# Which engine clears, rotates and sums, and when weights are split at the seams of a two-block network

## The chip, the core and the metric

The kernel runs on one core of one Trainium2 chip. Four engines compute: TensorE (PE, matmuls), VectorE (DVE), ScalarE (ACT) and GpSimd (POOL); SyncE (SP) issues most of the DMAs that bring the weights. The metric is the device time of one execution in microseconds (us). Three runs of the kernel before took 1218.33, 1220.27 and 1220.82 us.

## The reference, cut to what matters

256 tokens of width 1024 pass through two blocks in fp32. The first is modulated by a condition, the second has a gated linear attention (GLA), a differential attention and two MLPs.

```python
mod = silu(cond) @ w_mod + b_mod            # 9 groups of 1024: shift, scale, gate, three times
h = modulate(rms_norm(x, ffn1_norm), sh1, sc1)
x = x + 0.5 * g1 * swiglu(h, ffn1_w_gate, ffn1_w_up, ffn1_w_down)      # hidden width 2816
h = modulate(rms_norm(x, mix_norm), sh2, sc2)
b_gate, c_gate, v, u = split(h @ w_in)                                 # the mixer
y_conv = b_gate * causal_conv3(c_gate * v)
y_ssm = gelu(s5_scan(u))                     # complex diagonal state space, 32 groups of 64 states
y_ssm = y_ssm * sigmoid(y_ssm @ glu_w + glu_b)
x = x + g2 * (concat(rms_norm(y_conv), rms_norm(y_ssm)) @ w_out)
x = x + 0.5 * g3 * swiglu(modulate(rms_norm(x, ffn2_norm), sh3, sc3), ...)
h = rms_norm(x, final_norm)
h = h + gla_mixer(rms_norm(h, a_norm), ...)  # q, k, v, g, z = split(. @ w_in); chunk-wise decays
h = h + sqrelu_mlp(...)                      # hidden width 4096
h = h + diff_mixer(rms_norm(h, b_norm), k, v, ...)
h = h + sqrelu_mlp(...)
```

## The kernel before

**Matmuls.** Each fp32 matmul is made of three faster ones: an operand is split into a rounded part and the rest, and high by high, low by high and high by low are summed in PSUM. A weight comes in as a tile `stage` of 1 MB (128 x 2048, three tiles in turn). ScalarE casts it to `wh` in two instructions, VectorE takes `wl = stage - wh` in two instructions; both write one of four slots. These two lines (L185 and L187) are most of the work of both engines. A stage is free for the next DMA as soon as its `wl` is done, and SyncE's DMAs go out in the order of one list.

**The list.** `schedule` writes the order of all weights. `Stream.prep(upto)` splits the next ones as long as slots are free; `take` splits ahead before it hands out a weight, and its argument `ahead` limits how many are split at that place in the program. `w_mod`, the matrix of the modulation, runs in the same list but isn't split: VectorE multiplies it by the condition and adds up, two instructions of 1024 columns a megabyte into `macc` (L853 for the first product, L855 for the others), and TensorE then sums over partitions (`mod`, L876). `swap(n)` moves the last down weight of a feed-forward n places behind its natural place.

**Order of the stages.** Opening (norm of x, first two groups of the modulation, `evac_mod`, which scales and shifts the turned rows); ffn1 in 11 steps of 256 hidden columns (`up`, then `acc` for a step three back); the mixer; ffn2; GLA; MLP; diff; MLP. At a seam the last products of one stage are kept as a `Tail`: the sums of the first 128 tokens are added to x (`add_acc`, L398 and L399), normalised and turned (`xnT`) while TensorE does the second half's.

**GpSimd** clears tiles at the start (`Ssm.__init__`, L592 to L595), then computes small tables for the state space in a chain of many short operations (`prepare`, `powers`; later `readout` and `tables`). VectorE takes part in it with one reciprocal (L680). `Ssm.step` transposes the results on TensorE at ffn1's steps 2 to 4 (`s_end`), 7 to 9 (`s_lag`).

**Mixer.** Two rotations (`turning`, one for each half of the groups) turn the inputs of the scan, scan and turn back: 14 operations, eight on VectorE and six on GpSimd. Between them and after them stand the projections of the convolution and the outputs of the scan (`y`); then the first half of the output projection (`acc` from `s_tab`), the gate (`glu`), and the rest.

**GLA.** Decays for six levels of block sizes: `level_e` subtracts (`E`, on GpSimd), ScalarE takes exponentials, `level_x` multiplies q and k by them on VectorE, `level_mm` multiplies on TensorE; `across_e` does the same for whole chunks.

The order within each engine is that of the program's text; engines meet through semaphores alone.

Of the kernel before, what the change touches and what calls it, by code (L numbers as in the profile page):

```python
# [32 lines left out]
MODS_FFN1 = (2, 3, 4, 5, 6)  # L33
MODS_MIXER = (7,)
# [21 lines left out]
def schedule():  # L56
# [48 lines left out]
    swap(2)  # L105
    md = [4 * g + c for g in MODS_MIXER for c in range(4)]
    for c in (6, 7, 2, 4, 0, 3, 5, 1):
        w("w_in", c)
        if c in (0, 3, 5, 1):
            w("w_mod", md.pop(0))  # L110
# [25 lines left out]
class Stream:  # L136
# [63 lines left out]
    def take(self, name, j=0, ahead=10 ** 9):  # L200
        self.n_take += 1
        self.prep(self.n_take + ahead)
        W, slot = self.ready.pop((name, j))
        self.used.append(slot)
        return W


class Net:
# [219 lines left out]
    def turn(self, tail, evac, chunks, use):  # L428
# [57 lines left out]
    def ffn(self, tail, evac, ups, dn, steps, gated, post, side=None, n_first=3):  # L486
# [48 lines left out]
        for s in range(n_first, steps):  # L535
            res = []
            for u in ups:
                ps = self.bank_u("up")
                begins = s == n_first and u == ups[0]
                self.feat(self.take(u, s, 0 if begins else 10 ** 9), self.hT, v3(ps, 2))  # L540
# [23 lines left out]
        last = [(hd, self.take(dn, steps - 3 + n)) for n, hd in enumerate(pend)]  # L564
# [13 lines left out]
class Ssm:  # L578


    def __init__(self, N, p):
# [136 lines left out]
    def step(self, s):  # L718
# [3 lines left out]
        if 2 <= s <= 4:  # L722
            for b in ((0, 1), (2, 3, 4), (5, 6, 7))[s - 2]:
# [73 lines left out]
def build(N):  # L797
# [118 lines left out]
    ssm.powers()  # L916
# [32 lines left out]
    def side1(s):  # L949
# [5 lines left out]
    tail = N.ffn(None, lambda i: N.evac_mod(pts[i], i, modf[:, 1, :], modf[:, 0, :], N.hT),  # L955
                 ("ffn1_w_gate", "ffn1_w_up"), "ffn1_w_down", 11, True, post_ffn1, side1, 1)
# [4 lines left out]
        convw=sv["conv_w"], glub=sv["glu_b"], onorm=sv["out_norms"], ones=ones, xns=xns, mods=mods_ready))  # L961
# [87 lines left out]
def mixer(N, tail, evac, ssm, c):  # L1049
# [3 lines left out]
    vt, gt, act = nc.vector.tensor_tensor, nc.gpsimd.tensor_tensor, nc.scalar.activation  # L1053
# [31 lines left out]
    def proj(ch):  # L1085
        ps = N.bank_u("proj")
        N.feat(take("w_in", ch), N.hT, v3(ps, 2))
        N.S.free()
        return ps
# [30 lines left out]
    conv_v(0, vps)  # L1120
# [12 lines left out]
    def turning(h, m):  # L1133
# [90 lines left out]
    c["mods"]()  # L1224
# [59 lines left out]
def gla(N, tail, evac, c):  # L1284
    nc, t, t2, take = N.nc, N.t, N.t2, N.take
    ones, misc, ident = c["ones"], c["misc"], N.ident
    vt, gt, act = nc.vector.tensor_tensor, nc.gpsimd.tensor_tensor, nc.scalar.activation
# [28 lines left out]
    wz = [v3(w, KD) for w in take("a_z")]  # L1316
# [15 lines left out]
    for h2 in range(2):
        ps = N.bank_a("gate")
        for k in range(2):
            h = 2 * h2 + k
            nc.tensor.matmul(ps[:, S * k:S * k + S], wgu[:16, 128 * h:128 * h + 128], zT[:16, :], start=True, stop=True)
        gp.append(ps)
# [18 lines left out]
    def level_e(li):  # L1356
# [6 lines left out]
        gt(out=ev[:, :, 1, :], in0=bv[:, :, 1, :], in1=ref, op=SUB)  # L1363
        gt(out=ev[:, :, 0, :], in0=ref, in1=bv[:, :, 0, :], op=SUB)
# [51 lines left out]
    def across_e():  # L1416
# [8 lines left out]
        for i in range(2):  # L1425
            gt(out=ec[:, :, 2 * i, :], in0=tot(2 * i), in1=bc[:, :, 2 * i, :], op=SUB)
            nc.gpsimd.tensor_copy(out=ec[:, :, 2 * i + 1, :], in_=bc[:, :, 2 * i + 1, :])
        gt(out=e2[:, :, 0, :], in0=ec[:, :, 0, :], in1=tot(1), op=ADD)
        gt(out=e2[:, :, 1, :], in0=tot(1), in1=bc[:, :, 1, :], op=SUB)
        nc.gpsimd.tensor_copy(out=e2[:, :, 2, :], in_=bc[:, :, 2, :])  # L1430
        gt(out=e2[:, :, 3, :], in0=bc[:, :, 3, :], in1=tot(2), op=ADD)
# [29 lines left out]
    W = take("a_in", 7)  # L1461
    vt(out=kss[:, 2], in0=qf, in1=kf, op=MUL)
    level_x(0)
    level_e(2)
    exp(Es[2])
    level_x(1)
# [12 lines left out]
    W = take("a_in", 8)  # L1479
    level_x(2)  # L1480
    level_e(4)
    exp(Es[4])
    level_x(3)
# [5 lines left out]
    W = take("a_in", 9)  # L1489
# [11 lines left out]
    across()  # L1501
    for hd in range(3):
# [29 lines left out]
    for hp in range(2):  # L1532
        for i in range(2):
            av(i, hp)
    for hd in range(3):
        gated(hd)
    nc.scalar.preload_act_table(AF.Silu)
    W = take("a_in", 11)
    ps = N.bank_u("vg")
    for i in range(2):  # L1540
        N.tokm(W, N.hT, i, ps[:, CW * i:CW * i + CW])
    N.S.free()
    act(out=flat(sg[3]), in_=ps, func=AF.Silu)
# [63 lines left out]
def diff(N, tail, c):  # L1607
# [172 lines left out]
    queries(2)  # L1780
    turn_a(0)
    scores(1, N.bank_a)
    values(1)
    outputs(0)
    keys(3)
# [123 lines left out]
```

## Time and profile before

| | |
|---|---|
| median of three runs | 1220.27 us |
| profiled execution | 1219.3 us |
| its span | 1217.6 us |
| mean granted clock of TensorE | 0.959 |
| busy: PE, DVE, ACT, POOL | 1135.3, 793.7, 613.4, 236.6 us |
| bytes | 230 MB, 188 GB/s over the span |

The span is that of the instructions in the trace; the execution's time lies 1.7 us around it. "Busy" adds up the instructions' durations. A granted clock of 1 is 2.4 GHz, of 0.5 is 1.2 GHz; a stretch with a value between spent part of its time at each. In the list of waits the time stands against the instruction that ended the wait last. Roughly, the stages lie at: opening to 59 us, ffn1 to 262, mixer to 390, ffn2 to 590, GLA to 715, MLP to 920, diff to 1010, MLP to the end.

### The profile page before, as it was taken

To read this page: it belongs to the slowest core of one execution; us is meant where nothing else is said; L and a number is where in the kernel's file an instruction comes from. 1 tells how busy PE (TensorE), PEld (TensorE's weight loads), DVE (VectorE), ACT (ScalarE), POOL (GpSimd) and SP (SyncE) were. 2 spreads that over 40 slices of the span, in tenths; PEclk is the share of its full clock that TensorE was granted. 3 is DMA by queue.
4 is the path that set the end of the run, shared out by engine and by line. 5 is a ranking of instruction groups with operands and counts; after the bars stand their busy time and mean duration, and the time that the engine had idled before them with its cause. 6 is when DMAs were issued, how large, how long until landed. Compare 5 with 4: busy or idle time off the path is not lost.

```text
span 1217.6 us, 18757 instructions
## 1 busy us (share of the span) xinstructions
PE 1135.3 (93%) x7780; PEld 1051.7 (86%) x7780; DVE 793.7 (65%) x934; ACT 613.4 (50%) x941; POOL 236.6 (19%) x304
## 2 busy tenths in 40 slices
PE   1698999989789999999798999999999899999998
PEld 1697999979778999998798889999989897999997
DVE  7698797667968785565466665644468776564541
ACT  3444434455084554354364656655446764664541
POOL 8996399400500000000224100000000000000000
PEclk9698999989789999999897999999999899999999
DMA  8588787535243786565043245755625332385540
GB/s 318 225 327 308 249 322 281 202 139 208 88 155 139 260 324 213 189 242 181 30 144 135 90 141 202 251 178 199 205 107 194 118 118 108 124 291 194 183 143 35
DMA packets 33093, 230.13 MB, mean 189 GB/s; under 512 B 3680, under 2 KB 4064, under 8 KB 5872
## 3 DMA queue, kind: packets, MB, share of 16 engines
q1 hardware_dynamic: 31536, 224.05, 51.2%
q10 hardware_dynamic: 1472, 4.88, 1.1%
q8 instruction: 61, 1.00, 0.3%
q14 instruction: 24, 0.20, 0.0%
HBM read 227.87 MB, written 1.05 MB: 188 GB/s over the span
## 4 chain that ended last, share of the span: by engine, by line
PE 66%; DVE 16%; ACT 8%; POOL 4%; issue 3%; DMA 2%; ACTq 0%; DVEq 0%; POOLq 0%
PE acc L262 26%; PE up L262 25%; PE turn L262 7%; DVE wl L187 7%; ACT wh L185 2%; PE kqv L262 2%; DVE macc L855 1%; POOL s_small L626 1%; PE xnT L349 1%; POOL s_small L629 1%; PE lev L1385 1%; DMA stage<-in_ffn_w_up 1%; PE glu L262 1%; ACT s_lag L748 1%; POOL E L1363 1%
## 5 line engine op out<-in xcount | busy, mean ns | idle before, releaser
L187 DVE TENSOR_TENSOR wl<-stage,wh 128x1024 fp32r<-128x1024 f32 x351 | 425.7, 1261 | 131.3 <-ACT wh L185 131.1
L185 ACT CAST wh<-stage 128x1024 fp32r<-128x1024 f32 x351 | 346.8, 1045 | 126.1 <-PE acc L262 31.4
L262 PE MATMUL up<-hTh,wh 128*128 128x256 f32 x1024 | 289.2, 282 | 1.9 <-ACT s_end L729 1.9
L262 PE MATMUL up<-hTl,wh 128*128 128x256 f32 x1024 | 287.8, 281 | 0.0
L262 PE MATMUL up<-hTh,wl 128*128 128x256 f32 x1024 | 287.8, 281 | 0.0
L262 PEld LDWEIGHTS up<-hTh,wh 128*128 128x128 f32 x1024 | 193.9, 189 | 4.4 <-ACT s_end L729 2.3
L262 PEld LDWEIGHTS up<-hTh,wl 128*128 128x128 f32 x1024 | 196.2, 192 | 0.0
L262 PEld LDWEIGHTS up<-hTl,wh 128*128 128x128 f32 x1024 | 193.6, 189 | 1.5 <-issue 0.2
L262 PE MATMUL acc<-wh,hidh 128*128 128x512 f32 x288 | 115.0, 399 | 4.0 <-ACT wh L185 3.7
L262 PE MATMUL acc<-wl,hidh 128*128 128x512 f32 x288 | 114.0, 396 | 0.8 <-DVE wl L187 0.8
L262 PE MATMUL acc<-wh,hidl 128*128 128x512 f32 x288 | 113.9, 395 | 0.3 <-DVE hidl L296 0.3
L262 PE MATMUL turn<-wh,hTh 128*128 128x256 f32 x320 | 91.4, 286 | 6.2 <-ACT hTh L290 6.2
L262 PE MATMUL turn<-wl,hTh 128*128 128x256 f32 x320 | 90.9, 284 | 2.1 <-DVE wl L187 2.1
L262 PE MATMUL acc<-wh,macc 128*128 128x512 f32 x288 | 92.7, 391 | 0.0
L262 PE MATMUL turn<-wh,hTl 128*128 128x256 f32 x320 | 91.0, 285 | 0.2 <-DVE hTl L291 0.2
L855 DVE SCALAR_TENSOR_TENSOR macc<-stage,cact,macc 128x1024 f32<-128x1024 f32 x63 | 86.1, 1367 | 3.1 <-DMA stage<-in_w_mod 1.4
L262 PEld LDWEIGHTS acc<-wh,hidh 128*128 128x128 f32 x288 | 55.1, 191 | 15.5 <-ACT wh L185 4.1
L262 PEld LDWEIGHTS turn<-wh,hTh 128*128 128x128 f32 x320 | 61.3, 192 | 6.8 <-ACT hTh L290 6.5
L262 PEld LDWEIGHTS acc<-wh,hidl 128*128 128x128 f32 x288 | 54.9, 191 | 13.3 <-DVE hidl L296 1.0
L262 PEld LDWEIGHTS acc<-wl,hidh 128*128 128x128 f32 x288 | 55.0, 191 | 12.1 <-DVE wl L187 1.8
L262 PEld LDWEIGHTS turn<-wl,hTh 128*128 128x128 f32 x320 | 61.2, 191 | 3.1 <-DVE wl L187 2.8
L262 PEld LDWEIGHTS acc<-wh,macc 128*128 128x128 f32 x288 | 54.1, 188 | 11.0
(401 smaller groups left out, 2020.0 us busy)
## 6 DMA issues: line engine op xcount, KB each, us to landing
stage<-in_w SPq DMA_DIRECT2D x64, 1024.0 KB, 4.8
stage<-in_w_mod SPq DMA_DIRECT2D x36, 1024.0 KB, 4.9
stage<-in_ffn_w_gate SPq DMA_DIRECT2D x22, 1024.0 KB, 4.8
stage<-in_ffn_w_up SPq DMA_DIRECT2D x22, 1024.0 KB, 5.0
stage<-in_ffn_w_down SPq DMA_DIRECT2D x22, 1024.0 KB, 5.2
stage<-in_a_in SPq DMA_DIRECT2D x12, 1024.0 KB, 4.9
stage<-in_w_in SPq DMA_DIRECT2D x8, 1024.0 KB, 5.0
stage<-in_w_kv SPq DMA_DIRECT2D x8, 1024.0 KB, 4.9
```

The costliest lines, as they stand in the source:

```text
L185: nc.scalar.copy(out=h[:, b:e], in_=st[:, b:e])
L187: nc.vector.tensor_tensor(out=lo[:, b:e], in0=st[:, b:e], in1=h[:, b:e].bitcast(F32), op=SUB)
L262: self.nc.tensor.matmul(out, lhs(l, k), rhs(r, k), start=first and n == 0, stop=last and n == 3 * n_k - 1)
L349: self.nc.tensor.transpose(out, src, self.ident)
L626: g.tensor_tensor(out=o, in0=x, in1=y, op=op)
L629: g.tensor_scalar(out=o, in0=x, scalar1=s1, scalar2=s2, op0=op0, op1=op1)
L748: nc.scalar.copy(out=self.lag[32 * i:32 * i + 32, 4 * b:4 * b + 4, 32 * i:128], in_=ks[:32, :, 0:128 - 32 * i])
L855: nc.vector.scalar_tensor_tensor(out=acc, in0=wv[:, k, :], scalar=cc, in1=acc, op0=MUL, op1=ADD)
L1363: gt(out=ev[:, :, 1, :], in0=bv[:, :, 1, :], in1=ref, op=SUB)
L1385: nc.tensor.matmul(ps[:, 64 * e:64 * e + 64], ks[:, 128 * e:128 * e + 128], qs[:, 64 * e:64 * e + 64], start=True, stop=True)
```

## The change

The diff has these parts.

- Opening: the two clears of `s_out` go from GpSimd to VectorE, the clear of `s_lag` to ScalarE (an activation with scale 0), and `first` follows the clear of `p0`. `powers`, and with it the reciprocal, is called after the second evacuation. One weight's split goes between the two evacuations.
- Modulation: group 7 is loaded and multiplied in ffn1 instead of the mixer, one more megabyte in each of the steps 3 to 6. Its sum on TensorE goes along.
- `Ssm.step` transposes at steps 3 to 5, `readout` and `tables` follow step 5.
- Seams: the last weights of each feed-forward are taken with `ahead=0`, and `swap(2)` becomes `swap(1)`.
- Mixer: the rotation runs on VectorE alone; projections are issued between the two rotations; the first gelu comes after the gain splits.
- GLA: `level_e` and `across_e` subtract on VectorE (two copies go to ScalarE), splits are placed by explicit calls, and the last gate chunk is cut into halves around the products with v.
- Diff: the norms of the third and fourth heads' queries and keys come after the turned weights' copies.

```diff
-MODS_FFN1 = (2, 3, 4, 5, 6)
-MODS_MIXER = (7,)
+MODS_FFN1 = (2, 3, 4, 5, 6, 7)
...
-    swap(2)
+    swap(1)
...
         if tail is None:
             evac(0)
+            S.prep(S.n_take + 2)
             evac(1)
...
-        last = [(hd, self.take(dn, steps - 3 + n)) for n, hd in enumerate(pend)]
+        last = [(hd, self.take(dn, steps - 3 + n, 0)) for n, hd in enumerate(pend)]
...
-        self.first()
         g.memset(p0, 0.0)
         for c in range(2):
-            g.memset(self.out[c], 0.0)
-        g.memset(self.lag, 0.0)
+            N.nc.vector.memset(self.out[c], 0.0)
+        self.first()
+        N.nc.scalar.activation(out=self.lag, in_=N.ident.unsqueeze(1).to_broadcast([128, 16, 128]), func=AF.Copy, scale=0.0)
...
-        if 2 <= s <= 4:
+        if 3 <= s <= 5:
...
-        gt(out=m[0], in0=m[0], in1=m[1], op=ADD)
+        vt(out=m[0], in0=m[0], in1=m[1], op=ADD)
...
     turning(0, [t([512], "hm", bufs=2), t([512], "hm", bufs=2)] + pair(t([1024], "macc", bufs=2)))
+    conv_v(0, vps)
+    conv_b(0, proj(0))
+    conv_a(1, proj(3))
+    vps = proj(5)
     turning(1, [t([512], "hidh1"), t([512], "hidl1")] + pair(t([1024], "macc", bufs=2)))
-    conv_b(0)
-    conv_a(1, proj(3))
     outputs(0)
-    gelu(0)
-    conv_v(1, proj(5))
-    conv_b(1)
+    conv_v(1, vps)
+    conv_b(1, proj(1, 0))
     outputs(1)
...
-        gt(out=ev[:, :, 1, :], in0=bv[:, :, 1, :], in1=ref, op=SUB)
-        gt(out=ev[:, :, 0, :], in0=ref, in1=bv[:, :, 0, :], op=SUB)
+        vt(out=ev[:, :, 1, :], in0=bv[:, :, 1, :], in1=ref, op=SUB)
+        vt(out=ev[:, :, 0, :], in0=ref, in1=bv[:, :, 0, :], op=SUB)
...
-    queries(2)
+    new_norm("qn", 2)
+    ps = chunk("w_q", 2, hq)
     turn_a(0)
+    qk_norm(ps, [flat(nrm["qn", 2])])
```

VectorE's order at the end of the opening, before (`modf` is the finished shift or scale, `s_small` GpSimd's chain, `hm` and `hTl` the evacuation of one half of the tokens):

```order
L187 TENSOR_TENSOR wl<-stage,wh 128x1024 x2
L880 TENSOR_TENSOR modf<-mod,pack 128x8
L882 SCALAR_TENSOR_TENSOR modf<-modf,pack 128x8
L680 RECIPROCAL s_small<-s_small 128x16
L380 TENSOR_SCALAR hm<-xnT,modf 128x128 x4
L291 TENSOR_TENSOR hTl<-hm,hTh 128x4x128 x2
L380 TENSOR_SCALAR hm<-xnT,modf 128x128 x4
L291 TENSOR_TENSOR hTl<-hm,hTh 128x4x128 x2
L187 TENSOR_TENSOR wl<-stage,wh 128x1024 x2
```

And the same place now:

```order
L183 TENSOR_TENSOR wl<-stage,wh 128x1024 x2
L882 TENSOR_TENSOR modf<-mod,pack 128x8
L884 SCALAR_TENSOR_TENSOR modf<-modf,pack 128x8
L380 TENSOR_SCALAR hm<-xnT,modf 128x128 x4
L291 TENSOR_TENSOR hTl<-hm,hTh 128x4x128 x2
L183 TENSOR_TENSOR wl<-stage,wh 128x1024 x2
L380 TENSOR_SCALAR hm<-xnT,modf 128x128 x4
L291 TENSOR_TENSOR hTl<-hm,hTh 128x4x128 x2
L682 RECIPROCAL s_small<-s_small 128x16
```

The reciprocal has moved behind both evacuations, and the second weight's split between them.

VectorE at the end of the convolution in the mixer, before (`s_tab` is the scaled result that the output projection multiplies, `hTl` the rest of y, `rs_r` the reciprocal of the norm):

```order
L1110 TENSOR_TENSOR s_end_2887<-proj,hidl_3147 128x512
L296 SCALAR_TENSOR_TENSOR s_tab_3239<-s_end_2887,pack,s_tab_3238 128x256 x4
L291 TENSOR_TENSOR hTl<-s_ttmp,hTh 128x512
L1177 COPY s_tab_3250<-hidf 32x2x64 x6
L291 TENSOR_TENSOR hTl<-s_tab_3250,hTh 128x512
L880 TENSOR_TENSOR modf<-mod,pack 128x8
L882 SCALAR_TENSOR_TENSOR modf<-modf,pack 128x8
L187 TENSOR_TENSOR wl<-stage,wh 128x1024 x6
L305 RECIPROCAL rs_r_3346<-rs_sq 128x2
```

Now:

```order
L1115 TENSOR_TENSOR s_end_2893<-proj,hidl_3140 128x512
L296 SCALAR_TENSOR_TENSOR s_tab_3224<-s_end_2893,pack,s_tab_3223 128x256 x4
L1181 COPY s_ttmp<-hidf 32x2x64 x6
L291 TENSOR_TENSOR hTl<-s_ttmp,hTh 128x512
L1181 COPY s_tab_3253<-hidf 32x2x64 x6
L291 TENSOR_TENSOR hTl<-s_tab_3253,hTh 128x512
L183 TENSOR_TENSOR wl<-stage,wh 128x1024 x8
L305 RECIPROCAL rs_r_3346<-rs_sq 128x2
```

The finished shift of the modulation is gone from this place, and eight instructions of weight splits stand ahead of the reciprocal where six stood.

VectorE at the seam from ffn2 to GLA, before (`row` holds the gains of the final norm):

```order
L291 TENSOR_TENSOR hidl_5293<-hidf,hidh_5292 128x512
L187 TENSOR_TENSOR wl<-stage,wh 128x1024 x2
L187 TENSOR_TENSOR wl<-stage,wh 128x128
L187 TENSOR_TENSOR wl<-stage,wh 128x1024 x4
L398 SCALAR_TENSOR_TENSOR act<-acc,gate 128x512
L399 TENSOR_TENSOR x<-x,act 128x512
```

Now:

```order
L291 TENSOR_TENSOR hidl_5293<-hidf,hidh_5292 128x512
L183 TENSOR_TENSOR wl<-stage,wh 128x1024 x2
L398 SCALAR_TENSOR_TENSOR act<-acc,gate 128x512
L399 TENSOR_TENSOR x<-x,act 128x512
```

The splits of GLA's narrow weight (128 x 128) and of the next two weights have left the place between the last down weight's split and the sum.

## Rows read from the trace of the kernel before

**Rows 1.** Waits of PE, five of the list: us in total, times, longest.

```profile
PE y L1169 <- DVE xn L1151: 5.7, 1, 5.7
PE acc L262 <- ACT s_tab L295: 5.1, 1, 5.1
PE acc L262 <- ACT wh L185: 3.7, 1, 3.7
PE diag L1400 <- DVE ks L1462: 3.5, 1, 3.5
...
PE s L1698 <- ACT gate L1733: 3.1, 1, 3.1
```

**Rows 2.** Stretches: length, busy time of each engine, PEclk, DMA share, GB/s.

```profile
60.00:96.00 36.00, 35.13 (x244) 31.90 (x242) 33.97 (x27) 15.60 (x18) 35.12 (x27) 1.00 0.90 335
...
96.00:110.00 14.00, 10.05 (x54) 9.25 (x55) 13.08 (x12) 5.37 (x7) 13.44 (x14) 0.63 0.80 279
248.00:262.00 14.00, 9.63 (x30) 7.33 (x31) 8.16 (x10) 7.37 (x12) 0.00 (x0) 0.76 0.68 264
312.00:370.00 58.00, 46.76 (x296) 44.79 (x295) 46.98 (x60) 26.79 (x44) 16.11 (x17) 0.76 0.33 119
576.00:592.00 16.00, 8.86 (x43) 7.46 (x42) 11.41 (x19) 7.53 (x23) 0.00 (x0) 0.79 0.26 91
640.00:700.00 60.00, 55.24 (x396) 53.02 (x394) 39.79 (x50) 32.41 (x58) 16.48 (x16) 0.89 0.32 113
950.00:968.00 18.00, 13.88 (x86) 12.74 (x85) 13.99 (x29) 11.29 (x28) 0.00 (x0) 0.81 0.35 117
```

**Rows 3.** Timeline of DVE and ACT in the opening: start, duration, instruction, [idle before].

```profile
6.40 6.22 DVE L853 TENSOR_SCALAR macc<-stage,cact 128x1024 f32<-128x1024 f32 x1 [6.40 <-DMA stage<-in_w_mod]
12.65 9.21 DVE L855 SCALAR_TENSOR_TENSOR macc<-stage,cact,macc 128x1024 f32<-128x1024 f32 x7
...
23.83 0.73 DVE L853 TENSOR_SCALAR macc<-stage,cact 128x1024 f32<-128x1024 f32 x1
...
37.98 1.51 ACT L378 ACTIVATE hm<-xnT,modf 128x128 f32<-128x128 f32 x4 [2.82 <-DVE modf L882]
...
41.45 0.25 DVE L680 RECIPROCAL s_small<-s_small 128x16 f32<-128x16 f32 x1 [3.57 <-POOL s_small L626]
41.62 1.27 DVE L380 TENSOR_SCALAR hm<-xnT,modf 128x128 f32<-128x128 f32 x4
```

**Rows 4.** Timeline of POOL: the clears.

```profile
5.92 4.41 POOL L594 MEMSET s_out<- 128x2560 f32 x2
10.27 1.80 POOL L595 MEMSET s_lag<- 128x2048 f32 x1
```

**Rows 5.** SP's fourth request; DMA rate over 0 to 20 us, 0.5 us each.

```profile
13.96 0.33 SPq L156 DMA_DIRECT2D stage<-in_w_mod  x1
...
GB/s 0 0 0 31 388 49 115 442 426 410 442 426 393 442 442 410 442 410 442 442 377 442 442 410 459 311 0 0 0 115 66 180 393 442 459 360 361 344 426 426
```

**Rows 6.** Timeline of DVE and PE at the seam from ffn2 to GLA.

```profile
573.91 2.36 DVE L187 TENSOR_TENSOR wl<-stage,wh 128x1024 fp32r<-128x1024 f32 x2 [3.62 <-ACT wh L185]
576.19 0.68 DVE L398 SCALAR_TENSOR_TENSOR act<-acc,gate 128x512 f32<-128x512 f32 x1
...
584.08 1.94 PE L349 MATMUL xnT<-ident,xn 128*128 128x128 f32 x8 [7.14 <-DVE xn L995]
```

**Rows 7.** Timeline of DVE and POOL in the mixer's rotations.

```profile
308.15 0.69 DVE L1139 TENSOR_TENSOR hm<-ssm_w,s_tab 128x512 f32<-128x512 f32 x1
...
316.20 1.77 POOL L1150 TENSOR_TENSOR macc<-macc,s_tab 128x512 f32<-128x512 f32 x1 [1.16 <-DVE macc L1148]
...
318.44 0.68 DVE L1139 TENSOR_TENSOR hidh<-ssm_w,s_tab 128x512 f32<-128x512 f32 x1
```

**Rows 8.** Timeline of DVE in GLA: splits beside POOL's work, and without.

```profile
630.85 7.15 DVE L187 TENSOR_TENSOR wl<-stage,wh 128x1024 fp32r<-128x1024 f32 x4
...
640.96 4.74 DVE L187 TENSOR_TENSOR wl<-stage,wh 128x1024 fp32r<-128x1024 f32 x4 [2.96 <-ACT wh L185]
```

More of the change, by code (lines that the diff above doesn't have):

```diff
@@ L202, in take @@
         self.prep(self.n_take + ahead)
+        while (name, j) not in self.ready:
+            n = self.n_slot
+            self.prep(n + 1)
+            assert self.n_slot > n, (name, j)
         W, slot = self.ready.pop((name, j))
@@ L539, in ffn @@
                 begins = s == n_first and u == ups[0]
-                self.feat(self.take(u, s, 0 if begins else 10 ** 9), self.hT, v3(ps, 2))
+                ends = s == steps - 1 and u == ups[-1]
+                self.feat(self.take(u, s, 0 if begins or ends else 10 ** 9), self.hT, v3(ps, 2))
                 self.S.free()
@@ L954, in build, with evac_first @@
     tail_places("ffn1_w_down", 10, 0)
[L955 to L956 removed]
+    def evac_first(i):
+        N.evac_mod(pts[i], i, modf[:, 1, :], modf[:, 0, :], N.hT)
+        if i:
+            ssm.powers()
+    tail = N.ffn(None, evac_first, ("ffn1_w_gate", "ffn1_w_up"), "ffn1_w_down", 11, True, post_ffn1, side1, 1)
     mods_ready()
     tail = mixer(N, tail, evac_mod(1), ssm, dict(
[L961 removed]
+        convw=sv["conv_w"], glub=sv["glu_b"], onorm=sv["out_norms"], ones=ones, xns=xns))
     def after_mixer():
@@ L1083, in mixer, with proj @@
     cw = c["convw"]
-    def proj(ch):
+    def proj(ch, ahead=10 ** 9):
         ps = N.bank_u("proj")
-        N.feat(take("w_in", ch), N.hT, v3(ps, 2))
+        N.feat(take("w_in", ch, ahead), N.hT, v3(ps, 2))
         N.S.free()
@@ L1313, in gla @@
     nc.gpsimd.memset(step01.rearrange("p (n c) -> p n c", c=64)[:, :, 0:1], 0.0)
-    wz = [v3(w, KD) for w in take("a_z")]
+    wz = [v3(w, KD) for w in take("a_z", 0, 0)]
     zp = N.bank_u("z")[:16, :S]
@@ L1321, in gla, with featb, gates @@
     nc.vector.tensor_copy(out=zT[:16], in_=zp)
-    def featb(ch, dst, scale):
-        ps = N.bank_u("qk")
-        N.feat(take("a_in", ch), N.hT, v3(ps, 2))
+    def featb(ch, dst, scale, between=None, ahead=10 ** 9):
+        pv = v3(N.bank_u("qk"), 2)
+        wv = [v3(w, KD) for w in take("a_in", ch, ahead)]
+        for k in range(2):
+            cs = slice(128 * k, 128 * k + 128)
+            N.mm3(pv[:, k, :], lambda l, kk: wv[l][:, kk, cs], lambda r, kk: N.hT[r][:, kk, :], KD)
+            if k == 0 and between is not None:
+                between()
         N.S.free()
-        act(out=flat(dst), in_=ps, func=AF.Copy, scale=scale)
+        act(out=flat(dst), in_=flat(pv), func=AF.Copy, scale=scale)
     qT, kT = t2([4, S], "qT"), t2([4, S], "kT")
-    featb(0, qT[:, 0:2, :], 128 ** -0.5)
     gp = []
[L1332 to L1337, printed above, removed]
+    def gates():
+        N.S.prep(10 ** 9)
+        for h2 in range(2):
+            ps = N.bank_a("gate")
+            for k in range(2):
+                h = 2 * h2 + k
+                nc.tensor.matmul(ps[:, S * k:S * k + S], wgu[:16, 128 * h:128 * h + 128], zT[:16, :], start=True, stop=True)
+            gp.append(ps)
+    featb(0, qT[:, 0:2, :], 128 ** -0.5, gates, 0)
     e1, mn = t2([4, S], "E", bufs=2), t2([4, S], "E", bufs=2)
@@ L1460, in gla @@
     featb(3, kT[:, 2:4, :], 1.0)
-    W = take("a_in", 7)
+    W = take("a_in", 7, 0)
     vt(out=kss[:, 2], in0=qf, in1=kf, op=MUL)
     level_x(0)
+    level_x(1)
+    N.S.prep(10 ** 9)
     level_e(2)
     exp(Es[2])
-    level_x(1)
     level_e(3)
@@ L1477, in gate_chunk @@
         tok_chunk(8 + hd, [sg[hd][:, i, :] for i in range(2)], W)
-    W = take("a_in", 8)
+    W = take("a_in", 8, 0)
     level_x(2)
+    level_x(3)
+    N.S.prep(10 ** 9)
     level_e(4)
     exp(Es[4])
-    level_x(3)
     level_e(5)
@@ L1488, in gla @@
     level_mm(3)
-    W = take("a_in", 9)
+    W = take("a_in", 9, 0)
     level_x(4)
@@ L1494, in gla @@
         exp(E)
+    N.S.prep(10 ** 9)
     gate_chunk(1, W)
@@ L1501, in gla @@
     across()
+    W = take("a_in", 11)
+    last_gate = N.bank_u("vg")
+    N.tokm(W, N.hT, 0, last_gate[:, :CW])
     for hd in range(3):
@@ L1534, in gla @@
             av(i, hp)
+    N.tokm(W, N.hT, 1, last_gate[:, CW:])
+    N.S.free()
     for hd in range(3):
@@ L1537, in gla @@
     nc.scalar.preload_act_table(AF.Silu)
[L1538 to L1543, printed above, removed]
+    act(out=flat(sg[3]), in_=last_gate, func=AF.Silu)
     c["load"]("m0", t([D], "macc", bufs=2))
```

47 lines of the change are left out of this document (23 added, 24 removed).

## The prediction

> **What bounds the kernel now.** I read the list of TensorE's waits first, then the table of stretches, then the rows around each wait, and last the order of the instructions. TensorE is busy 93% of the span, so time can come only from its idle stretches and from the work it does at the lower clock. Nearly all its idle time behind the opening stands in single waits [rows 1]: the reader is to see that each happened once, so each is one place of the program, and that a VectorE or ScalarE instruction which prepares the next stage ends it, not a DMA.
>
> The stretches around these waits also run at a lower granted clock [rows 2]. A clock of 0.76 over 58 us (312 to 370) means 2 x 0.24 x 58 = 27.8 us at 1.2 GHz and the rest at 2.4. With I the idle time (length less PE's busy time) and h the time at 1.2 GHz, a stretch loses I + (h - I)/2 if all its idle time fell into h, and I + h/2 if none did. So 96-110 loses 7.2 to 9.1 us, 248-262 5.5 to 7.7, 312-370 19.5 to 25.1, 576-592 6.9 to 10.5, 640-700 9.0 to 11.4, 950-968 5.5 to 7.5. That is the whole stock, some 54 to 71 us, beside the opening. The change touches each of these places.
>
> **Opening.** VectorE's first product takes 6.22 us, the same instruction later 0.73 [rows 3]. It starts at 6.40 and ends at 12.62, half a microsecond behind GpSimd's last clear (10.27 + 1.80 = 12.07) [rows 3, 4]. The change puts the two large clears on VectorE, which is idle until 6.40, and the third on ScalarE, idle there too. On VectorE their price isn't in the trace: 4.4 us on GpSimd for both [rows 4], and 3.7 by VectorE's product of 1024 columns (5 x 0.73). With nothing ahead of them either ends before 6.40; the bad end, clears that wait for GpSimd as the product did, is the third rival. ScalarE's clear is a fifth of that work, where ScalarE has nothing until x has landed at 13 [rows 5]. The first eight products then need 0.73 + 9.21 = 9.9 us and not 15.4, but their fourth megabyte is requested when the first stage is free: 13.96 before [rows 5], 8.4 now (6.40 + 0.73 + 9.21/7). It lands behind x, whose bytes end at 13 in the row of the DMA rate; at that row's 430 GB/s or so a megabyte takes 2.45 us, so at about 16, an estimate. The products then end 2.6 later, about 18.7 and not 21.86: 3.2 us earlier, not 5.5. The second eight follow and keep the 3.2.
>
> The Trainium skill (SBUF — State Buffer, section SBUF: two separate sides) says that VectorE and GpSimd share one port pair as an exclusive lock: the loser waits for the whole instruction. The rows agree: 12.62 - 12.07 is about the bare product. By that rule the clears on VectorE hold up GpSimd's first small operations in turn; GpSimd starts its long chain at about 6 instead of 12.16 even so, and no term here would change.
>
> Then the reciprocal: at 41.45 VectorE waits 3.57 us for GpSimd in front of the shift and scale that TensorE needs [rows 3]; behind the second evacuation it stops nobody. What is late next is ScalarE's half of the same evacuation: it ended at 39.49 (37.98 + 1.51), VectorE's at 42.89, so 3.4 us are won. Both together: the first "turn" starts 6.6 us earlier. Bounds: 3.4 (if the clears keep the products where they were) to 9 (if the second weight's split between the two evacuations removes its own short wait too). I take **6.6**.
>
> **ffn1, third to sixth step.** TensorE waits at 97 for tables that GpSimd writes to s_out; that stretch, 96-110, loses 7.2 to 9.1 us [rows 2]. The transposes that read them come one step of some 17 us later now, and GpSimd starts its chain 6 us earlier. I take 8 as gone. Against it stand eight more products of the modulation in steps 3 to 6, two each: 1.29 us each alone (9.21 / 7), up to 1.6 beside GpSimd, 2.6 to 3.2 a step. VectorE was busy 33.97 of 36 us at 60-96 [rows 2], so weights come just in time and the lead that the old stall gave is missing. I book 2 us of new waits (bounds 0 and 9, next part). The reduction on TensorE that goes with the eight products only moves from the mixer to ffn1. Net **6.0**.
>
> **Seam ffn1 to mixer.** The load of the last down weight goes out three items earlier, so the 3.7 us wait for its split goes with its half clock: 6.6 (middle of 5.5 and 7.7). But the split of w_in 7, two instructions of VectorE, 2.36 us as in [rows 6], now stands ahead of the second half's sum, and behind that sum are its norm, TensorE's transposes and the evacuation. I let 4.2 come back. **2.4**, bounds -2 and 6.
>
> **Mixer.** Removed from VectorE: eight products, some 10 us, and the waits for GpSimd inside the rotation (its line is called turning). Six of the 14 operations of each rotation come over from GpSimd: 0.69 on VectorE, 1.77 on GpSimd [rows 7]; 14 x 0.69 make 9.7 us, the rotation took 10.3 with GpSimd's help (308.15 to 318.44), so it costs nothing. Between the rotations three projections are issued for TensorE, which waited 5.7 us for the first rotation and 5.1 for the last gain split [rows 1]. These 10.8 go, and 8.3 of half clock with them (27.8 less the stretch's 11.2 idle, halved). What is late next: VectorE splits four weights in a row, 4 x 2.36 = 9.4 us, ahead of the reciprocal and of the scaling that the second product of the output projection and the next norm wait for; before it was three of them, and the reduction's result in between. Behind these splits stand the reciprocal, the sigmoid's products, the gain splits and both sums. I book 8.5 us of new waits, and 1.6 as lost since the rotations meet projections that fill TensorE only partly: **9**, bounds 0 and 17.
>
> **Seam ffn2 to GLA.** Before, the sum at 576.19 stands behind a split that waited 3.62 us for ScalarE, and TensorE idles 7.14 us for the normalised rows behind it [rows 6]. In the new order only the last down weight's split is ahead. The sum of the second column half can start when TensorE has closed that bank, about 571.3, an estimate (TensorE ended at 576.94, and 24 of the tail's 60 matmuls, two fifths of some 14 us, belong to the other token half), instead of 578.25 (576.19 + 3 x 0.69): 6.9 us earlier, so TensorE hardly waits. With part of the half clock (6.9 to 10.5 in all) **8**, bounds 5 and 9.4.
>
> **GLA.** Twelve subtractions of 512 columns and six small ones come to VectorE or ScalarE: 12 x 0.68 and about 2, some 10 us. VectorE gets back what the neighbour cost it: four splits took 7.15 us beside GpSimd and 4.74 without [rows 8], and I double these 2.4 for the other places where both worked. So VectorE carries 5 more in a stretch of 60 where it was busy 39.8 [rows 2], and the exponentials no longer wait for GpSimd. TensorE's 3.5 us for the diagonal go, and half of the clock loss. From 9.0 to 11.4 I take **5**, bounds -4 and 9.
>
> **Diff.** The key norm no longer stands ahead of the copies of the turned weights which TensorE awaits 3.1 us [rows 1]. Of 5.5 to 7.5 I take **2.5**, bounds 0 and 5.
>
> Sum: 6.6 + 6.0 + 2.4 + 9 + 8 + 5 + 2.5 = 39.5. The profiled execution took 1219.3 us (span 1217.6); 1179.8 by its count. The median shown is 1.0 above it, so the forecast is 1181.
>
> **Rivals.** First, weights run out in ffn1. At the pace of 60-96 VectorE needs 15.8 us for a step of 16.75 (33.97/36); with 3.1 more 18.9, that is 2.1 short in each of four steps, 8.6 in all, with half clock behind the waits about 11.5 instead of 2: 1190. For it: VectorE's 94% there. Against it: GpSimd pauses between 110 and 145, and VectorE has room.
>
> Second, VectorE becomes the bound where it took GpSimd's work: the four splits hold the mixer so that it gains 2 and not 9, and GLA loses 1 and not wins 5: 1194. For it: VectorE was already busy 47.0 of 58 us in the mixer. Against it: 9.9 us of products left that stretch.
>
> Third, the opening doesn't do what it says: VectorE's clears start late or run at GpSimd's pace or slower, and products and chain stand where they stood: 1181 + 6.6 = 1188.
>
> Fourth, the slower side: VectorE falls behind from the second step of ffn1 to its end, so that every step ends in a wait and the lower clock follows it. The rows show some 6.8 us at 1.2 GHz behind a single wait (2 x 0.19 x 18), which costs 3.4; with 2.1 of wait a step loses 5.5, nine steps 49.5, less the 2 that are booked: 1181 + 47.5 = 1228. It turns the sign from 4.6 us a step on. Against it: only four steps get more work.
>
> **Numbers.** The forecast 0.62 (its own range 1168 to 1187), weights run out 0.14, VectorE the bound 0.14, opening unchanged 0.05, no change by compensation 0.01, slower 0.04. 0.2% is 2.4 us, about what a measurement of this kernel tells from none. Faster 0.95, same 0.01, slower 0.04. The low end is the better ends of mixer and GLA together (8 + 4) and some of the rest: 1164. The high end takes in both middle rivals and part of their sum: 1203.
>
> **What would show it.** Right: the first product near 0.75 us, the first projection of ffn1 ("turn") 6 us or more earlier, no reciprocal in front of the evacuation; no wait for s_out; y and the gain split no longer among TensorE's waits; transposes behind ffn2 without a wait above 1 us. Wrong: new waits of "up" or "acc" for wl at 75 to 150; a wait of several us for the sigmoid's or the gain split's result behind four splits; VectorE over 90% busy in GLA. The forecast falls if the sum of TensorE's waits behind the opening stays above 30 us.

## The result, and the profile after

The changed kernel takes 1199.58 us (median of four runs, 1198.46 to 1200.53), the one before 1219.8 beside it: a ratio of 0.9833, 95% interval 0.9817 to 0.9848. The profiled execution's span is 1197.8 us, 19.8 less. The forecast was 39.5 less: the direction is right, the size half.

The first instruction of each stage on TensorE, in the timelines of both traces, shows where the 39.5 went. "Lead" is how much earlier the changed kernel starts there, "stage gave" what the stage that ends at the row added to the lead.

| TensorE starts | before | after | lead | stage gave | forecast |
|---|---|---|---|---|---|
| ffn1, `up` of s=1 | 59.26 | 51.62 | 7.6 | opening 7.6 | 6.6 |
| ffn1, `up` of s=3 | 102.19 | 86.66 | 15.5 | | |
| ffn1, `up` of s=4 | 122.38 | 106.91 | 15.5 | | |
| ffn1, `up` of s=6 | 158.23 | 158.86 | -0.6 | | |
| ffn1, `up` of s=10 | 230.33 | 231.42 | -1.1 | ffn1 -8.7 | 6.0 |
| mixer, `uT` | 287.72 | 290.05 | -2.3 | seam -1.2 | 2.4 |
| ffn2, `up` of s=2 | 415.31 | 406.05 | 9.3 | mixer 11.6 | 9 |
| GLA, `z` | 608.96 | 591.07 | 17.9 | ffn2 and seam 8.6 | 8 |
| MLP, first `up` | 740.57 | 722.00 | 18.6 | GLA 0.7 | 5 |
| diff, first `kqv` | 924.22 | 909.44 | 14.8 | MLP -3.8 | 0 |
| diff, `o` | 968.34 | 948.46 | 19.9 | diff 5.1 | 2.5 |

TensorE's waits, from the list of the changed kernel (total, times, longest), against [rows 1]:

```profile
PE s_end L349 <- DVE hidf L478: 6.1, 1, 6.1
PE diag L1414 <- DVE ks L1476: 5.8, 1, 5.8
PE acc L262 <- ACT wh L181: 4.1, 2, 2.5
PE up L262 <- DVE hidf L478: 3.7, 2, 2.2
PE glu L262 <- ACT rs_sq L303: 3.1, 1, 3.1
...
PE up L262 <- ACT s_end L731: 1.8, 1, 1.8
...
PE s L1715 <- ACT gate L1750: 0.7, 1, 0.7
...
PE y L1173 <- DVE xn L1155: 0.4, 1, 0.4
```

The waits for the gain split (5.1) and, but for 0.4 and 0.7, for y (5.7) and the turned weights (3.1) are gone, as forecast. The diagonal's is longer than its 3.5. New or much longer are those for `hidf`, ffn1's gated product, and for the mixer's square root.

In sum little went. From the `up` of s=1 to the end TensorE was busy 1112.0 of 1158.3 us before and is busy 1100.5 of 1146.2 now: 46.4 us idle became 45.7. The 12 us won behind the opening are nearly all in the busy time of the same instructions. By the mean granted clocks of the two whole spans, 0.959 and 0.974, TensorE spent some 100 us at 1.2 GHz before and some 62 now (an estimate: twice the missing share of each span).

The opening went nearly as worked out: the first `turn` starts at 37.71 instead of 43.59, 5.9 us earlier for 6.6 forecast, and ffn1 gets 7.6. VectorE's timeline, beside [rows 3, 4]; the last two rows are GpSimd's:

```profile
1.41 2.19 DVE L595 MEMSET s_out<- 128x2560 f32 x1 [1.41 <-PEq L1924]
4.08 2.19 DVE L595 MEMSET s_out<- 128x2560 f32 x1 [0.48 <-issue]
6.29 0.75 DVE L855 TENSOR_SCALAR macc<-stage,cact 128x1024 f32<-128x1024 f32 x1
...
16.09 2.60 DVE L857 SCALAR_TENSOR_TENSOR macc<-stage,cact,macc 128x1024 f32<-128x1024 f32 x2 [2.08 <-DMA stage<-in_w_mod]
...
44.69 0.25 DVE L682 RECIPROCAL s_small<-s_small 128x16 f32<-128x16 f32 x1
...
4.71 0.22 POOL L614 TENSOR_TENSOR s_small<-pack,s_small 128x16 f32<-128x16 f32 x1 [2.24 <-ACT s_small L613]
...
45.08 0.22 POOL L680 TENSOR_TENSOR s_small<-s_small 128x16 f32<-128x16 f32 x1 [9.26 <-DVE s_small L682]
```

The clears take 2.19 us each, as on GpSimd, and end before the first product, which takes 0.75 instead of 6.22. The first eight products end at 18.69 (forecast 18.7), held up by the fourth megabyte. The forecast let the clears on VectorE hold up GpSimd's first small operations; the two at 4.71 and 4.89 took 0.22 us each inside VectorE's second clear, and no term rested on it. But GpSimd now idles 9.26 us for the reciprocal: the 6 us that its chain had won are lost again, and its last copy of the tables for `s_end` ends at 107.8 instead of 99.2.

The stretch that lost, from the table of stretches (columns as in [rows 2]; the kernel before at 110 to 130 stands behind it) and the timelines of VectorE and TensorE:

```profile
52.00:94.00 42.00, 40.73 (x295) 37.67 (x293) 38.93 (x30) 16.08 (x19) 40.98 (x34) 1.00 0.90 328
...
110.00:130.00 20.00, 16.61 (x120) 15.22 (x119) 18.60 (x15) 7.87 (x10) 10.20 (x9) 1.00 0.90 341
130.00:145.00 15.00, 8.91 (x53) 8.54 (x54) 10.61 (x11) 5.86 (x8) 0.00 (x0) 0.66 0.90 343
```

```profile
110.00:130.00 20.00, 20.00 (x155) 19.00 (x154) 14.07 (x14) 10.40 (x14) 1.42 (x2) 1.00 0.77 277
```

```profile
131.42 0.75 DVE L855 TENSOR_SCALAR macc<-stage,cact 128x1024 f32<-128x1024 f32 x1 [1.47 <-DMA stage<-in_w_mod]
132.21 1.28 DVE L857 SCALAR_TENSOR_TENSOR macc<-stage,cact,macc 128x1024 f32<-128x1024 f32 x1
133.41 0.69 DVE L478 TENSOR_TENSOR hidf<-up,act 128x512 f32<-128x512 f32 x1
```

```profile
134.24 1.09 PE L349 MATMUL s_end<-ident,s_out 128*128 128x128 f32 x4 [6.13 <-DVE hidf L478]
137.17 0.58 PE L262 MATMUL up<-hTh,wh 128*128 128x256 f32 x1 [1.84 <-ACT s_end L731]
```

The up product of s=4 ended at 120.05 and its `hidf` started 13.4 us later, behind splits and products, one of which also waited 1.47 us for its megabyte. TensorE's next transposes, the third block of s=4, waited for `hidf`; the clock was at its lower level for 10.2 us (0.66 over 130 to 145), and the whole lead of 15.5 us was spent by the start of s=6.

### The profile page after: what moved, and what is told of

It reads as the page before. It is cut to its first block, busy times and chain, and to the rows that moved or that the text cites. A ratio compares the mean times of both kernels' runs of the same rounds, so it can differ in the third digit from the quotient of the medians.

```text
span 1197.8 us, 18746 instructions
## 1 busy us (share of the span) xinstructions
PE 1123.0 (94%) x7780; PEld 1039.3 (87%) x7780; DVE 796.8 (67%) x963; ACT 615.7 (51%) x945; POOL 192.1 (16%) x271
## 4 chain that ended last, share of the span: by engine, by line
PE 64%; DVE 19%; ACT 9%; DMA 4%; issue 3%; ACTq 0%; DVEq 0%
PE acc L262 24%; PE up L262 24%; PE turn L262 8%; DVE wl L183 8%; ACT wh L181 3%; DVE macc L857 2%; DMA stage<-in_w_mod 2%; PE vg L262 2%; PE kqv L262 1%; PE lev L1399 1%; PE xnT L349 1%; DMA stage<-in_ffn_w_up 1%; DVE x L399 1%; DVE act L398 1%; ACT s_lag L750 1%
## 5 line engine op out<-in xcount | busy, mean ns | idle before, releaser
L262 PEld LDWEIGHTS acc<-wh,hidh 128*128 128x128 f32 x288 | 54.7, 190 | 13.9 <-ACT wh L181 2.9
```

The costliest lines, as they stand in the source:

```text
L262: self.nc.tensor.matmul(out, lhs(l, k), rhs(r, k), start=first and n == 0, stop=last and n == 3 * n_k - 1)
```

## The experiments

Each ran three rounds beside the kernel before; the ratio stands with its interval. "Lead" is the lead of a stage's start in the run's trace over that of the kernel before, as in the table; it is read from one execution. Where an edit lies in another stage, a stage's gain wanders by itself: in the mixer from 10.8 to 11.6 us, in GLA from 0.0 to 1.6, in diff from 2.0 to 5.3, in ffn1 from -8.5 to -11.0, at the seam behind ffn1 from -1.2 to -1.9. Three theories for ffn1: order (A), amount (B), GpSimd beside VectorE (C).

**Third megabyte behind the down weight (e1).**

```diff
+            if s - first < 8:
+                w(pre + "_w_down", s - first)
             if s > 2 and len(md) > 2 * (10 - s):
                 w("w_mod", md.pop(0))
-            if s - first < 8:
-                w(pre + "_w_down", s - first)
```

> The changed kernel, with the third megabyte of the modulation in each of ffn1's steps 3 to 6 (and wherever else there is one) placed behind the step's down weight in the list instead of ahead of it; same bytes, same instructions. Between the fourth and the sixth step the changed kernel loses 16 us against the one before. Theory A (order): the two products of that megabyte stand ahead of the gated product hidf in VectorE's queue, wait there for their DMA, and TensorE waits for hidf; then 8 to 14 us come back, 1186 to 1192 us, and TensorE's waits for hidf (9.8 us in all) fall under 3. Theory B (amount): VectorE and the three stages can't deliver six megabytes a step, wherever they stand; then 1198 to 1201 and the waits only change their names. Theory C (neighbour): GpSimd's chain, which now ends 9 us later than before, slows VectorE's instructions in these steps; then also 1198 to 1201.

Measured 1199.25 us, 0.9819 (0.9782 to 0.9857): unchanged. A falls as the whole cause. In the trace TensorE's waits for `hidf` fell from 9.8 to 3.2, and a wait of 3.2 for the activation ahead of it came. The profiled execution is an outlier, 1192.46 beside timed runs of 1198.5 to 1200.6: the 2.5 us wait at the last down weight was absent in it. It is absent too in run e12, which contains this edit and whose profiled execution is again the fastest. What decides that is open.

**Additional megabytes at steps 7 to 10 (e2).** `if s > 2` becomes `if s > 6`.

> The changed kernel, with the four additional megabytes of the modulation taken in ffn1's steps 7 to 10 instead of 3 to 6. A and B: the steps 3 to 6 are relieved and the later ones have room (VectorE 75% busy at 180 to 248 in both kernels), so 10 to 15 us come back: 1185 to 1190. C: VectorE is slowed at steps 3 and 4 all the same, so at most 4: 1196 or more. Bad case for A and B: GpSimd's tables, now at steps 6 to 10, slow VectorE there and the loss only moves: 1195.

Measured 1200.01, 0.9834 (0.9807 to 0.986). The lead at s=6 is 10.1 us, at s=10 it is -3.3. So the steps 3 to 6 are relieved, as A and B say, and the loss moves to the later ones: the bad case in full. TensorE pays the debt in one wait, where VectorE works beside GpSimd's tables: four products took 8.21 us there, at 1.28 each alone they take 5.1, and the activation that ended the wait stood behind a cast that waited 7.31 us for the step's down weight:

```profile
233.61 0.58 PE L262 MATMUL up<-hTh,wh 128*128 128x256 f32 x1 [8.70 <-ACT act L477]
```

**Group 7 back in the mixer (e3).** `MODS_FFN1 = (2, 3, 4, 5, 6)`, `MODS_MIXER = (7,)`, its loads and its sum as before.

> The changed kernel, with group 7 of the modulation back in the mixer as before (its four megabytes between the projections, its sum in front of the gate). A and B: ffn1 ends some 14 us earlier than in the changed kernel, at the start of the tenth step 13 us ahead of the kernel before. The mixer pays for it with 10 us of products on VectorE, 5 to 10 of which TensorE sees: 1191 to 1197 in all. C: ffn1 unchanged within 3 us and the mixer worse: 1204 or more.

Measured 1204.27, 0.987 (0.9844 to 0.9896), 4.7 us slower than the changed kernel, with intervals that just touch. ffn1 is 10.0 us better at s=10 (lead 8.95), so group 7 costs that there. The mixer turns a lead of 6.8 into 4.6, where the changed kernel wins 11.6: TensorE waits 9.6 us for y again. B holds for most of the loss, but a lead of 16.0 at s=3 still falls to 9.1 by s=6 without group 7.

**Reciprocal after the first evacuation (e4).** `if i:` becomes `if not i:` ahead of `ssm.powers()`.

> The changed kernel, with VectorE's reciprocal for GpSimd behind the first evacuation instead of the second. GpSimd idles 9.3 us for that reciprocal in the changed kernel; it now comes 5 to 6 us earlier, and the whole chain with it (last copy into s_out at 102 instead of 108). C: VectorE is free of its neighbour earlier, and 3 to 6 us of the loss at steps 4 and 5 come back: 1194 to 1197. A and B: the waits for hidf hang on the modulation's megabytes, so within 2 us of 1199.6. The evacuation itself pays 0.25 us at most.

Measured 1201.17, 0.9842 (0.9811 to 0.9873). GpSimd's wait fell to 2.5 us and its last copy into s_out ended at 98.9 instead of 107.8, and ffn1 didn't change (lead -1.35 at s=6), though GpSimd was busy only 2.7 of 20 us at 110 to 130 instead of 10.2. C falls as far as GpSimd's lateness goes. That GpSimd slows VectorE at all stays: in the changed kernel a pair of splits takes 2.89 us at 100.6 beside it and 2.36 at 125.1.

**Group 7 without seven of its products (e5).** `w = 8 if g == 7 else D` columns.

> The changed kernel, but of the eight products of group 7 seven cover 8 columns instead of 1024: the shift of ffn2 is left out but for these, the four megabytes are loaded as before. It parts what the earlier runs left together in the amount theory B. B1 (VectorE's time): without these 9 us of VectorE the stretch from the fourth to the tenth step of ffn1 gets back the 10 us that group 7 costs there, as it did when the group went to the mixer; 1187 to 1191 us. B2 (stages and DMA): the megabytes still pass through the three stages, so ffn1 keeps its loss within 3 us: 1196 to 1200.

Measured 1195.19, 0.9805 (0.9788 to 0.9821). The lead at s=10 is -1.4, as after: but group 7 is the list's last, so these products lie in the last steps, and the run doesn't part B1 from B2. What it shows is the seam: 4.2 us won there instead of 1.2 lost. The last products cost the seam some 5 us.

**Third megabytes without products (e9).** `w = 8 if 4 * g + c in (14, 17, 20, 23) else D`.

> The changed kernel, but of the third megabyte in each of ffn1's steps 3 to 6 (groups 3, 4 and 5 of the modulation) seven of eight products cover 8 columns instead of 1024; the loads stay. The run without group 7's products took them away in steps 9 and 10, where the group lies in the list, and so did not test the stretch that loses. B1 (VectorE's time): 9 us less for VectorE at the fourth to sixth steps bring 6 to 10 us back by the start of step 7; 1190 to 1194. B2 (three stages, some 5 us from request to landing each): the loss at these steps stays within 3 us; 1197 to 1200.

Measured 1197.77, 0.9819 (0.9788 to 0.9851). The loss from s=3 to s=6 falls from 16.2 us to 12.0: 4.2, less than B1's 6, while the loss that is left is far above B2's 3. VectorE was spared some 7 us and not 9, since each small product still takes 0.23 instead of 1.28. With group 7's loads gone too the same loss is 7.0 (run e3): so some 5 us more go with the loads, and 7.0 stand without either. The table of stretches of this run, and VectorE ahead of the same `hidf`:

```profile
110.00:130.00 20.00, 14.29 (x104) 13.13 (x103) 15.13 (x14) 8.19 (x11) 6.40 (x7) 0.89 0.98 386
```

```profile
128.14 0.75 DVE L855 TENSOR_SCALAR macc<-stage,cact 128x1024 f32<-128x1024 f32 x1 [2.03 <-DMA stage<-in_w_mod]
128.93 0.23 DVE L858 SCALAR_TENSOR_TENSOR macc<-stage,cact,macc 128x8 f32<-128x8 f32 x1
129.07 0.68 DVE L478 TENSOR_TENSOR hidf<-up,act 128x512 f32<-128x512 f32 x1
```

With VectorE relieved, 15.1 of 20 us busy instead of 18.6, the DMAs are busy 98% of the time and VectorE waits 2.0 us for a megabyte in front of `hidf`. So here VectorE and the loads bind within a few us of each other.

**The MLPs' last weights ahead again (e6).** In the two calls of `take` with `ahead=0` that the change added to the feed-forward, the limit holds only for the gated ones (ffn1, ffn2); the MLPs get `10 ** 9` again.

> The changed kernel with the last weights of the two MLPs split ahead again as before; ffn1 and ffn2 as changed. The first MLP's last weight is requested at 867.75 in the changed kernel, since a stage is held by a weight that waits to be split, and TensorE waits 2.4 us for it and loses the clock. Theory: the 3.8 us which the changed kernel loses between the first MLP and diff are that; 1195 to 1197. Rival: they come from diff's first weights; unchanged at 1198 to 1201.

Measured 1195.61, 0.981 (0.9795 to 0.9825). The lead is 19.9 us at the MLP's start and 19.9 at `kqv`: the 3.8 us are back to the tenth. The theory holds.

**Two weights ahead of the gates (e7).** `N.S.prep(10 ** 9)` becomes `N.S.prep(N.S.n_take + 2)` in `gates`.

> The changed kernel with two weights split ahead of GLA's gate products instead of all that find a slot (four). From the gate's matmuls to the cumulated decays b the changed kernel takes 20 us, the one before 13, since the gate's four sums stand behind eight split instructions on VectorE and wait for a DMA at 601. Theory: that eats the gain of GLA (0.3 us there instead of the 5 forecast); the sums start 5 us earlier, the diagonal's wait of 5.8 us goes, 1192 to 1196. Rival: VectorE's additional subtractions bind; then the wait moves to a later place and the time stays within 2 us of 1199.6.

Measured 1204.46, 0.9873 (0.9851 to 0.9896): slower. VectorE between the gates and the diagonal's products, first in the changed kernel, then in this run:

```profile
614.35 2.29 DVE L1361 TENSOR_TENSOR_SCAN b<-gate,E 128x1024 f32<-128x1024 f32 x1
616.55 4.61 DVE L183 TENSOR_TENSOR wl<-stage,wh 128x1024 fp32r<-128x1024 f32 x4
...
627.90 1.22 DVE L1476 TENSOR_TENSOR ks<-qT,kT 128x1024 f32<-128x1024 f32 x1
```

```profile
610.17 2.29 DVE L1361 TENSOR_TENSOR_SCAN b<-gate,E 128x1024 f32<-128x1024 f32 x1
612.38 6.88 DVE L183 TENSOR_TENSOR wl<-stage,wh 128x1024 fp32r<-128x1024 f32 x6
620.65 2.36 DVE L183 TENSOR_TENSOR wl<-stage,wh 128x1024 fp32r<-128x1024 f32 x2 [1.39 <-ACT wh L181]
...
629.76 1.22 DVE L1476 TENSOR_TENSOR ks<-qT,kT 128x1024 f32<-128x1024 f32 x1
```

The decays come 4 us earlier, and the splits put off stand behind them instead: `ks` is 1.9 later. (1.0 of the 4 is this run's earlier start of `z`.) TensorE's wait for the diagonal falls from 5.8 to 4.8 and a new one of 1.9 for a split comes ahead of it. The theory falls, and so does the rival's number, within 2 us. By VectorE's timeline fourteen split instructions stand between `z` and `ks` in both, eight and six in the changed kernel, four and ten here: the queue ahead of the diagonal keeps its length. Some 3 us of the slower time are diff's (below).

**Three splits ahead of the mixer's gate (e8).** `take("glu_w")` becomes `take("glu_w", 0, 2)`.

> The changed kernel with three splits instead of four ahead of the mixer's gate (the fourth, ffn2's first weight, comes later). In the changed kernel that fourth cast waits 2.4 us for its DMA on ScalarE, ahead of the square root and two table loads that TensorE's gate product waits for (3.1 us, then 1.3). Theory: 3 to 6 us come back between the gate and ffn2: 1194 to 1197. Rival: the split is missing later at ffn2's first projection, which then waits as long; 1198 to 1202.

Measured 1202.68, 0.9858 (0.9835 to 0.9881). The square root came 3.5 us earlier and TensorE's wait for it went, but the next seam waited 2.1 us more for the norm; the mixer gains 13.8 instead of 11.6. That is less than the theory's 3 to 6, and the time is nearer the rival's; again some 3 us of it are diff's.

**GLA's level sums back on GpSimd (e10).** `vt` becomes GpSimd's `tensor_tensor` in `level_e`.

> The changed kernel with GLA's twelve level subtractions back on GpSimd; the rest of GLA in the new order. Forecast's theory: they cost TensorE 2 us each as exponentials wait for them, 3 to 6 us in all: 1203 to 1206. Rival (the run with fewer splits before the gates pointed to it): between the gates and the diagonal VectorE and ScalarE have a fixed amount of splits, and the subtractions on VectorE only join that queue; within 2 us of 1199.6.

Measured 1207.8, 0.9888 (0.9859 to 0.9916). Of the 8 us over the changed kernel's 1199.6, GLA takes 2.8 (its lead falls from 13.1 to 11.0 where the changed kernel's rises by 0.7). This run already starts `z` 4.8 later, for reasons ahead of the edit. Beside GpSimd four splits take 7.14 us again and one subtraction 4.99:

```profile
621.65 7.14 DVE L183 TENSOR_TENSOR wl<-stage,wh 128x1024 fp32r<-128x1024 f32 x4
```

```profile
637.13 4.99 POOL L1377 TENSOR_TENSOR E<-b 128x512 f32<-128x512 f32 x1 [7.44 <-DVE ks L1390]
```

So the move is worth some 2 to 4 us, at the low end of the forecast's theory, given how GLA's gain wanders; the time itself is above both texts' ranges by what lies ahead of the edit.

**Rotation back on GpSimd (e11).** `vt` becomes GpSimd's in six lines of `turning`.

> The changed kernel with the six operations of each rotation back on GpSimd; the new order of the mixer stays. Forecast's theory: the rotation itself costs the same on either side, and the gain of the mixer is that of the projections between the rotations and of the products that left: within 2 us of 1199.6. Rival: the operations on GpSimd wait at each hand-over and slow VectorE's beside them, TensorE gets y later and waits again for it: 1203 to 1208.

Measured 1202.63, 0.9855 (0.9825 to 0.9884). The mixer gains 10.8 by the trace instead of 11.6, no less than in other traces without this edit, and TensorE waits 2.3 us in all for y instead of 0.6. The time is 1 us outside the theory's 2, its interval overlaps the changed kernel's. So the engine makes at most a small part of the mixer's gain. That the order of the projections makes it is not shown: with the new order kept and only group 7 back, the mixer loses 2.3 (run e3), and no run takes the order back alone.

**Four edits together (e12).** The tails, the third megabyte's place, three splits, and:

```diff
-        if 3 <= s <= 5:
-            for b in ((0, 1), (2, 3, 4), (5, 6, 7))[s - 3]:
+        if 3 <= s <= 6:
+            for b in (2 * s - 6, 2 * s - 5):
...
-            if s == 5:
+            if s == 6:
```

> The changed kernel with four edits together: the MLPs' last weights ahead as before (3.8 us by the run alone), the third megabyte behind the down weight (0 by times, 7 in one profile), three splits before the mixer's gate (1), and the transposes of the s_out tables two blocks a step over steps 3 to 6 instead of two, three and three over 3 to 5, so that no block waits for a PSUM bank that hidf still reads (2.3 to 6 us of wait at step 5 in all runs, with half clock behind it). If the wait at step 5 is that of the third block: 1185 to 1192. If VectorE is late there for any block: 1192 to 1196.

Measured 1196.37, 0.9798 (0.9766 to 0.983); with the tails alone 0.981 (0.9795 to 0.9825). Both beat the kernel before and can't be told apart; against the changed kernel's 0.9817 to 0.9848 both intervals overlap, that of the tails alone by a hair. The profiled execution, 1191.84, is the fastest of this run. In it TensorE's wait of 6.1 us at the transposes of s=4 has become one of 2.7 and the lead at s=6 is 6.8, but `readout`, a step later now, isn't done when its result is wanted:

```profile
194.78 0.63 PE L741 MATMUL s_lag<-s_out,s_tab 128*32 128x128 f32 x2 [5.06 <-POOL s_out L769]
```

and the lead at s=8 is -2.9. In this combination the third block's wait went, and GpSimd's took its place.

## Why the prediction was right in direction and twice too large

**Opening, mixer, ffn2's seam**: right, 27.8 us measured for 23.6 forecast. The steps named there (products at 18.7, the reciprocal out of the evacuation, projections between the rotations, the sum ahead of the other splits) all show in the trace. In the mixer the sum came right, its parts are not told apart: group 7's leaving is worth 13.9 us there (run e3), more than the whole gain. (The products' 1.29 us are misdivided, 9.21 / 7 is 1.32; nothing hangs on it.)

**The sign of failing** that the forecast named, TensorE's waits behind the opening above 30 us in sum, came true: TensorE's idle time there was 46.4 us and is 45.7. Of the waits that it counted those for y, for the gain split, for the norm behind ffn2 and for the turned weights went; those for the diagonal and the last down weight stayed, and it booked too few new ones.

**ffn1** is the step that failed: "I take 8 as gone ... I book 2 us of new waits". Measured -8.7 instead of 6.0, most of the difference of 19.7. The forecast read the stop at 97 to 107 as a wait for GpSimd's tables. TensorE's rows of the kernel before say that this was only its first part, and VectorE's row which `hidf` was due:

```profile
97.48 1.12 PE L349 MATMUL s_end<-ident,s_out 128*128 128x128 f32 x4 [2.35 <-POOL s_out L712]
99.16 1.11 PE L349 MATMUL s_end<-ident,s_out 128*128 128x128 f32 x4 [0.56 <-DVE hidf L477]
102.19 0.58 PE L262 MATMUL up<-hTh,wh 128*128 128x256 f32 x1 [1.91 <-ACT s_end L729]
```

```profile
98.43 0.68 DVE L477 TENSOR_TENSOR hidf<-up,act 128x512 f32<-128x512 f32 x1
```

The second block of transposes waited for `hidf`, not for GpSimd; by these rows it would have stood there until 99.1 with the tables ready. VectorE, busy 33.97 of 36 us just before, was in debt: by the timelines `hidf` started 10.7 and 10.5 us after its `up` at s=1 and 2, and 0.4 after it at s=3, when the stop had passed. In the changed kernel, without that stop, it starts late at s=2 and 3 and at s=4 (133.41, above):

```profile
94.19 0.68 DVE L478 TENSOR_TENSOR hidf<-up,act 128x512 f32<-128x512 f32 x1
...
113.58 0.68 DVE L478 TENSOR_TENSOR hidf<-up,act 128x512 f32<-128x512 f32 x1
```

That is 14.3, 12.7 and 13.4 us behind its `up`, until TensorE has to stop at the transposes again and the clock falls with it. The first rival saw VectorE's shortage and gave it 11.5 us and a chance of 0.14; the loss from s=4 to s=6 is 16.1. Group 7 accounts for 10.0 of the lead at s=10 (run e3), as both VectorE's time and loads (run e9); it is not the order of one product (run e1) nor GpSimd's later chain (run e4). The 7.0 that go without group 7 are open between the debt, which stays at 9.5 to 11.3 us through s=4 in that run, and the three blocks of transposes at s=4; no run puts the old stop back. Even so the group is better off here than in the mixer, by 4.7 us.

**Seam ffn1 to mixer**: -1.2 instead of 2.4. The last down weight's wait fell only from 3.7 to 2.5, and group 7's last products cost some 5 us there (run e5), which the text booked nowhere. The new wait for the second half's norm, for which 4.2 were booked, is 2.2.

**GLA**: 0.7 instead of 5. The sums' move is worth some 2 to 4 (run e10). What failed is "TensorE's 3.5 us for the diagonal go": the wait rose to 5.8, with fourteen split instructions between `z` and `ks` wherever eight or four of them stand ahead of the gates' sums (run e7). Nor did "half of the clock loss" go: from `z` to the MLP the granted clock is 0.93 and was 0.94. VectorE carries 7 us more there, forecast 5.

**MLP**: -3.8, booked at nothing. `ahead=0` acts on every feed-forward's last weights. In the MLP it holds a staged weight back, and with it the stage that the last weight's DMA needs (run e6).

**Diff**: 5.1 instead of 2.5. Two terms make it up, the second not certain: the wait for the copies, and the clock (last section).

## What to carry to other kernels

Ahead of taking a wait away, ask what would have stopped the engine next at the same place, and how late the producers already are: a wait of the bounding engine is also time in which the engines that feed it catch up, and here, with one of them 94% busy, it came back two steps later. Add up the waits that are left, too, and not only those that went. Compare, step by step, when a consumer's input is ready and when it is used; a wait list shows only the debts that have fallen due. An argument that is changed inside a shared helper for one stage is to be followed through all its callers.

## What the runs showed of the hardware beyond that

The same stretch of diff, with TensorE equally busy, ran at full clock in the changed kernel and partly at 1.2 GHz in the run with two weights ahead of the gates, whose code there is the same:

```profile
930.00:948.00 18.00, 16.44 (x131) 15.66 (x130) 14.32 (x28) 12.66 (x29) 0.00 (x0) 1.00 0.35 118
```

```profile
935.00:953.00 18.00, 16.44 (x105) 15.29 (x104) 13.94 (x28) 12.66 (x31) 0.00 (x0) 0.81 0.33 117
```

The second run reaches this code 2.1 us later, and its window is moved by 5; moved by 2.1 it has the same busy time and clock. TensorE's waits are 0.88 and 0.69 us in both. The second takes diff's gain from 5.1 to 2.2 us, so identical waits may or may not cost the clock, and single traces of this kernel differ by some 3 us there. At the start of `z` the run with the sums on GpSimd, whose code ahead of it is that of the changed kernel, stands 4.8 us behind it. That is about what separates several runs above.
